# Block products of a SwiGLU layer: two of seven put between ordinary products, side work moved away from the other five

## The chip, the cores and the metric

The kernel runs on one core of one Trainium2 chip. The metric is the device time of one execution in microseconds (us); lower is better.

## The reference

One layer of a decoder, 256 tokens of width 2048, all in 32-bit floats. The change touches only its second half, the feed-forward part:

```python
def swiglu(h, w_ffn_in, w_ffn_out):
    gate, up = jnp.split(h @ w_ffn_in, 2, axis=-1)
    return (jax.nn.silu(gate) * up) @ w_ffn_out
...
    mod = jax.nn.silu(c) @ w_ada[l] + b_ada[l]
    shift1, scale1, gate1, shift2, scale2, gate2 = jnp.split(mod[:, None, :], N_MOD, axis=-1)
...
    h = rms_norm(x, norm2_gain[l]) * (1 + scale2) + shift2
    x = x + gate2 * swiglu(h, w_ffn_in[l], w_ffn_out[l])
```

The inner width D_FF is 5632: w_ffn_in is 2048 by 11264 (5632 gate columns, then 5632 up columns), w_ffn_out is 5632 by 2048. `gate2`, one of six modulation vectors, is a product of one row with a large matrix and is computed beside the feed-forward part.

## The kernel before

**Matrix products.** Every float is split into a high and a low half that TensorE takes (`fp32r`), and a product is made of three matmuls (`mm3`): high weights with high activations (L170), low weights with high activations (L171), high weights with low activations (L172). Weights move in tiles of two chunks of 128 rows by 512 columns, 512 KB. One tile goes through three steps: a load on SyncE's queue (L159, `raw_tile`, into a ring of four `raw` buffers, with two more, tags A4 and A8, in FFN-in, or four, H4 to H7, in FFN-out); a cast on ACT to the high half (L166, `whi`); a subtraction on DVE for the low half (L167, `wlo`). `whi` and `wlo` are rings of four, so that a new half can be made when TensorE has done with the one four tiles earlier. `block` multiplies chunks k0 to k1 into two banks, one for each tile of 128 tokens (`NT` = 2): twelve matmuls for each weight tile.

**FFN-in.** The loop runs over i=0 to 10 (`NFF` = 11). Each step makes 512 gate columns (`pg`, two banks) and 512 up columns (`pu`, two banks) from 16 chunks of 128 (`KC`). In step 0 all of it is ordinary. From i=1 on the first four chunks of gate and up together are done as a 2x2 block product in seven products in place of eight, `right_sums` for the weights' side and `chain` for the rest. With c11, c21 the two token tiles of the gate and c12, c22 those of up, the products stand in this order, each of six matmuls: P1 into c11 (weights b11); P2 into a bank of its own, `side` (t1 = b12-b11); after them ACT copies c11 to c21 (L1268) and `side` to `held` (L1271); P3 into c21 (t2 = b22-t1); DVE sets c12 = c21 + held (L1252); P4 into c11 (b21); P5 into c21 (b22-b12); DVE sets c22 = c21 + held (L1252); P6 into c12 (b22); P7 into c21 (b21-t2). On the activations' side the sums (`h2_sums`, `total`) are ready. Then `block` adds chunks 4 to 15 of the gate to pg, ACT takes Silu (L1307), `block` adds chunks 4 to 15 of up to pu, and DVE multiplies the two (L1315). I call the part from P1 to Silu the gate half, the rest the up half.

**FFN-out.** Four column blocks of 512 (n=0 to 3) over 44 chunks (`KF`), in pairs n=0/1 and n=2/3. The first eight chunks of a pair are two groups of block products (`act_sums`, two entries), so that each of the seven products has twelve matmuls; the rest is ordinary.

**Side work**, in three kinds. Transposes: each step's product of gate and up is turned for FFN-out by `turn` (eight transposes on TensorE, L1071; a cast on ACT, L190; a subtraction on DVE, L191), kept in `later` and issued in the next step between P5 and P6; `block` would issue it as well, when it comes to its chunk `DEFER` = 4 with `later` filled. The second gate's multiply-adds: a tile of 128 by 1024 of `ada_rest` is loaded by SP (L371) into a ring of three buffers (tags AR0, AR1, KC) and added by DVE (L287), 32 of them; then the bias rows (`rows_of`: loads of `b_ada`, L935, into a ring `scr` of three; DVE, L936; high and low halves in T6, L945 and L946; matmuls with a row of ones, L950/L951; a copy, L952). These are steps of a generator, which `tick` advances: `block` calls `tick(state["rate"])` once a weight tile, and the rate is RATE_FFN = 0.4 all through FFN-in. Left sums: at i=8 and 9 (`LATE`) the sums of activations that FFN-out's block products need (`left_sums`, L1207 to L1214, on DVE but for a cast on ACT).

**What sets the order.** The program is written in order and a scheduler orders each engine's queue by priorities. `prio()` moves what stands in it ahead by `AHEAD` = 4000 places, so the weights' loads, casts and low halves go as early as their buffers allow. `tc.issue_after(x)` keeps an instruction behind x. Each engine then works its list strictly in order.

Of the kernel before, what the change touches and what calls it, by code (L numbers as in the profile page):

```python
# [67 lines left out]
def trunk(ctx: ExitStack, tc: tile.TileContext, I, out):  # L68
# [16 lines left out]
    def S(tag, shape, dtype=F32):  # L85
        return slot.tile(shape, dtype, tag=tag, name=nm(tag))
# [1130 lines left out]
    def right_sums(src, b0, b1, places):  # L1217
# [6 lines left out]
        def differ(tag, x, y):  # L1224
            d = S(tag, [P, 2, NB])
            nc.vector.tensor_tensor(d, x, y, op=ALU.subtract)
            return d

        out = []
        with prio():  # L1230
            raws = [(raw_tile(src, 4 * g, b0), raw_tile(src, 4 * g, b1)) for g in range(len(places))]
            raws = [r + (raw_tile(src, 4 * g + 2, b0), raw_tile(src, 4 * g + 2, b1)) for g, r in enumerate(raws)]
            out += [halved(b11) for b11, b12, b21, b22 in raws]
            t1 = [differ(p[0], r[1], r[0]) for p, r in zip(places, raws)]
            out += [halved(t) for t in t1]
            t2 = [differ(p[1], r[3], t) for p, r, t in zip(places, raws, t1)]
            out += [halved(t) for t in t2]
            out += [halved(r[2]) for r in raws]
            out += [halved(differ(p[0], r[3], r[1])) for p, r in zip(places, raws)]
            out += [halved(r[3]) for r in raws]  # L1240
            for t, r in zip(t2, raws):
                nc.vector.tensor_tensor(t, r[2], t, op=ALU.subtract)
            out += [halved(t) for t in t2]
        return out

    def chain(lefts, sums, rights, c11, c21, c12, c22):

        side, held = misc_bank([P, NB]), scr([P, NB])
# [5 lines left out]
        rights = iter(rights)  # L1254

        def product(ps, left, first=False):
            for g in range(len(sums)):
                hi, lo = next(rights)
                for i in range(2):
                    h, l = left(g, i)  # L1260
                    begin, end = first and g == i == 0, g == len(sums) - 1 and i == 1
                    mm3(ps, h, l, hi[:, i, :], lo[:, i, :], begin, end, seeded=True)

        total = lambda q: lambda g, i: (sums[g][0][:, q, i, :], sums[g][1][:, q, i, :])
        part = lambda c, t: lambda g, i: lefts(4 * g + c + i, t)
# [11 lines left out]
        if later:  # L1277
            with tc.issue_after(state["mm"].ins), prio():
                later.pop()()
        product(c12, total(3))  # L1280
        product(c21, part(2, 1))
# [148 lines left out]
```

## Time and profile before

| | |
|---|---|
| median of 3 runs | 1637.32 us (1631.86 to 1638.42) |
| profiled execution | 1637.97 us, span 1636.2 us |
| granted TensorE clock, mean | 0.991 |
| TensorE busy | 1598.8 us, 98% of the span, 7269 instructions |
| DVE busy | 1240.3 us, 76%, 1418 instructions |
| ACT busy | 854.5 us, 52%, 1180 instructions |
| GpSimd busy | 5.3 us |
| read from memory | 393.71 MB, 243 GB/s over the span |

Busy TensorE time is the time in which any matmul was on its way; matmuls overlap, so that a busy engine need not be at its peak, and the distance between starts tells more. A row of the profile's timeline gives start, length, engine, line, operation, output <- inputs, shape, count, and in brackets the idle time ahead with what ended it. Lines are those of this kernel; in the changed kernel those from L1307 on are four higher.

### The profile page before, as it was taken

The numbers are of one execution on the slowest core, as the hardware profiler recorded it, in microseconds if no ns is written. First come the engines' busy times: TensorE is split into PE (matmuls) and PEld (weight loads), VectorE is DVE, ScalarE is ACT, GpSimd is POOL, SyncE is SP. The second block draws the span as 40 slices with busy tenths as digits, with TensorE's granted clock in tenths as the row PEclk, the third lists the DMA queues.
The fourth block names the chain that finished last, engine by engine and source line by source line (L and its number), as shares of the span: only waits on it lengthen the run. The fifth ranks groups of instructions, "written<-read, shape, count | busy, mean of one in ns | idle before, by whom it ended". The sixth has DMA issues, their size and how long they took to land.

```text
span 1636.2 us, 20051 instructions
## 1 busy us (share of the span) xinstructions
PE 1598.8 (98%) x7269; PEld 1313.2 (80%) x7269; DVE 1240.3 (76%) x1418; ACT 854.5 (52%) x1180; POOL 5.3 (0%) x14
## 2 busy tenths in 40 slices
PE   8999999999999999999999999999999998999999
PEld 7878888788777888888887887888787786788787
DVE  6889996878779787878757778888888775755754
ACT  5654458755677444444445555555555553544532
POOL 1000000000000000000000000000000000000000
PEclk9999999999999999999999999999999998999999
DMA  8999996875767889888676577777775566666653
GB/s 332 352 327 319 328 314 210 295 249 151 237 217 242 276 304 312 304 309 305 223 217 220 155 256 239 244 259 239 263 224 184 172 205 223 198 202 181 206 155 114
DMA packets 116179, 399.24 MB, mean 244 GB/s; under 512 B 13090, under 2 KB 13896, under 8 KB 116080
## 3 DMA queue, kind: packets, MB, share of 16 engines
q1 hardware_dynamic: 115856, 397.95, 73.7%
q8 instruction: 57, 0.93, 0.2%
q14 instruction: 42, 0.34, 0.1%
q0 software_dynamic: 224, 0.01, 0.0%
HBM read 393.71 MB, written 4.19 MB: 243 GB/s over the span
## 4 chain that ended last, share of the span: by engine, by line
PE 87%; DVE 6%; DMA 3%; ACT 2%; issue 1%; POOL 0%; DVEq 0%; ACTq 0%; POOLq 0%
PE acc L172 26%; PE acc L171 26%; PE acc L170 26%; DVE wlo L167 3%; DMA AR<-ada_rest 1%; ACT whi L166 1%; PE acc L430 1%; PE misc L786 1%; PE misc L170 1%; PE misc L171 1%; PE misc L1071 1%; PE misc L172 1%; DVE ada L287 1%; DMA raw<-w_in 0%; PE misc L423 0%
## 5 line engine op out<-in xcount | busy, mean ns | idle before, releaser
L166 ACT CAST whi<-raw 128x1024 fp32r<-128x1024 f32 (+1 forms) x449 | 459.9, 1027 | 486.8 <-PE acc L172 376.7
L167 DVE TENSOR_TENSOR wlo<-raw,whi 128x1024 fp32r<-128x1024 f32 (+1 forms) x449 | 531.4, 1191 | 233.0 <-ACT whi L166 231.2
L171 PE MATMUL acc<-wlo,H 128*128 128x512 f32 x1476 | 579.2, 392 | 6.1 <-DVE wlo L167 6.0
L172 PE MATMUL acc<-whi,H 128*128 128x512 f32 x1476 | 578.5, 392 | 0.9 <-DVE H L1157 0.5
L170 PE MATMUL acc<-whi,H 128*128 128x512 f32 x1476 | 577.0, 392 | 0.8 <-ACT H L1156 0.4
L171 PEld LDWEIGHTS acc<-wlo,H 128*128 128x128 f32 x1476 | 278.2, 188 | 66.9 <-DVE wlo L167 10.5
L172 PEld LDWEIGHTS acc<-whi,H 128*128 128x128 f32 x1476 | 278.2, 189 | 59.6 <-DVE H L449 1.8
L170 PEld LDWEIGHTS acc<-whi,H 128*128 128x128 f32 x1476 | 278.3, 189 | 58.3 <-ACT H L442 1.2
L166 ACT CAST whi<-A 128x1024 fp32r<-128x1024 f32 x98 | 103.0, 1054 | 94.8 <-PE acc L172 86.5
L170 PE MATMUL acc<-whi,A 128*128 128x512 f32 x332 | 131.4, 397 | 7.6 <-ACT whi L166 5.6
L167 DVE TENSOR_TENSOR wlo<-A,whi 128x1024 fp32r<-128x1024 f32 x98 | 118.7, 1218 | 24.1 <-ACT whi L166 24.1
L171 PE MATMUL acc<-wlo,A 128*128 128x512 f32 x332 | 129.9, 391 | 0.0
L172 PE MATMUL acc<-whi,A 128*128 128x512 f32 x312 | 122.6, 393 | 0.0
L287 DVE SCALAR_TENSOR_TENSOR ada<-AR,csil,ada 128x1024 f32<-128x1024 f32 x59 | 74.9, 1279 | 8.1 <-DMA AR<-ada_rest 8.1
L170 PEld LDWEIGHTS acc<-whi,A 128*128 128x128 f32 x332 | 62.6, 189 | 22.3 <-ACT whi L166 6.1
L166 ACT CAST whi<-H 128x1024 fp32r<-128x1024 f32 x41 | 43.0, 1053 | 64.0 <-PE acc L172 39.4
L167 DVE TENSOR_TENSOR wlo<-H,whi 128x1024 fp32r<-128x1024 f32 x41 | 49.8, 1221 | 35.0 <-ACT whi L166 34.9
L171 PEld LDWEIGHTS acc<-wlo,A 128*128 128x128 f32 x332 | 62.6, 189 | 12.6 <-DVE wlo L167 0.4
L172 PEld LDWEIGHTS acc<-whi,A 128*128 128x128 f32 x312 | 59.2, 190 | 12.4
L171 PE MATMUL acc<-wlo,T 128*128 128x512 f32 x120 | 46.7, 389 | 0.0
L170 PE MATMUL acc<-whi,T 128*128 128x512 f32 x120 | 46.7, 389 | 0.0
L172 PE MATMUL acc<-whi,T 128*128 128x512 f32 x120 | 46.7, 389 | 0.0
(407 smaller groups left out, 1560.4 us busy)
## 6 DMA issues: line engine op xcount, KB each, us to landing
raw<-w_in SPq DMA_DIRECT2D x203, 512.0 KB, 4.9
raw<-w_ffn_in SPq DMA_DIRECT2D x122, 512.0 KB, 4.4
AR<-ada_rest SPq DMA_DIRECT2D x79, 512.0 KB, 4.8
A<-w_ffn_in SPq DMA_DIRECT2D x54, 512.0 KB, 4.7
raw<-w_ffn_out SPq DMA_DIRECT2D x53, 512.0 KB, 4.2
H<-w_ffn_out SPq DMA_DIRECT2D x35, 512.0 KB, 4.0
raw<-w_out SPq DMA_DIRECT2D x32, 512.0 KB, 4.6
KC<-ada_rest SPq DMA_DIRECT2D x30, 512.0 KB, 5.3
```

Of the source, the lines that this page charges most:

```text
L166: nc.scalar.copy(hi, raw)
L167: state["split"] = nc.vector.tensor_tensor(lo, raw, hi.bitcast(F32), op=ALU.subtract)
L170: nc.tensor.matmul(ps, lh, rh, start=start, stop=False, skip_group_check=seeded)
L171: nc.tensor.matmul(ps, lh, rl, start=False, stop=False, skip_group_check=seeded)
L172: state["mm"] = nc.tensor.matmul(ps, ll, rh, start=False, stop=stop, skip_group_check=seeded)
L287: nc.vector.scalar_tensor_tensor(acc, raw, c, acc, op0=ALU.mult, op1=ALU.add)
L430: state["warm"] = nc.tensor.matmul(ps, ones_r, wide, start=True, stop=True)
L786: nc.tensor.matmul(ps[:n, t * N_GLA + h, :].rearrange("p (s l) -> p s l", l=L), at(f, h, t)[:, :n], odd(at(f, h, t)), start=True, stop=True,)
L1071: nc.tensor.transpose(ps[:, i, :], src[:, i * P : (i + 1) * P], ident)
```

## The change

`paired` takes the place of `right_sums` and `chain`. The first five products stand as before. P6 and P7 each get an ordinary weight tile of the gate ahead of them: chunks 4 and 5, P6, chunks 6 and 7, P7, then chunks 8 to 15. In FFN-out with its two groups each of the four half products gets one: chunks 8 and 9 to 14 and 15. The transposes are no longer issued between P5 and P6; the last `block` of `paired` issues them when it has done four chunks, so behind chunks 8 to 11. The rate of the side work is 0.8 a weight tile within `paired` for i below 7 (six tiles a step), 1.6 from i=7 on, and 0 in the up half; before it was 0.4 for twelve tiles. The left sums come after all of `paired` in the program. As the rate is doubled from i=7, all of the last bias rows' work falls in i=7 to 9. The number of matmuls and of DVE, ACT and SP instructions stays what it was.

```diff
@@ -1214,55 +1214,55 @@
         nc.vector.tensor_tensor(lo, raw, hi.bitcast(F32), op=ALU.subtract)
         return hi, lo
 
-    def right_sums(src, b0, b1, places):
+    def paired(act, sums, places, src, b0, b1, p0, p1, k1):
+
+        (c11, c21), (c12, c22) = p0, p1
+        n = len(sums)
+        side, held = misc_bank([P, NB]), scr([P, NB])
 
         def halved(raw):
             hi, lo = halves_room()
             halve(hi, lo, raw)
             return hi, lo
 
-        def differ(tag, x, y):
-            d = S(tag, [P, 2, NB])
+        def differ(x, y, tag=None, into=None):
+            d = S(tag, [P, 2, NB]) if into is None else into
             nc.vector.tensor_tensor(d, x, y, op=ALU.subtract)
             return d
 
-        out = []
         with prio():
-            raws = [(raw_tile(src, 4 * g, b0), raw_tile(src, 4 * g, b1)) for g in range(len(places))]
+            raws = [(raw_tile(src, 4 * g, b0), raw_tile(src, 4 * g, b1)) for g in range(n)]
             raws = [r + (raw_tile(src, 4 * g + 2, b0), raw_tile(src, 4 * g + 2, b1)) for g, r in enumerate(raws)]
-            out += [halved(b11) for b11, b12, b21, b22 in raws]
-            t1 = [differ(p[0], r[1], r[0]) for p, r in zip(places, raws)]
-            out += [halved(t) for t in t1]
-            t2 = [differ(p[1], r[3], t) for p, r, t in zip(places, raws, t1)]
-            out += [halved(t) for t in t2]
-            out += [halved(r[2]) for r in raws]
-            out += [halved(differ(p[0], r[3], r[1])) for p, r in zip(places, raws)]
-            out += [halved(r[3]) for r in raws]
-            for t, r in zip(t2, raws):
-                nc.vector.tensor_tensor(t, r[2], t, op=ALU.subtract)
-            out += [halved(t) for t in t2]
-        return out
-
-    def chain(lefts, sums, rights, c11, c21, c12, c22):
-
-        side, held = misc_bank([P, NB]), scr([P, NB])
+            first = [halved(r[0]) for r in raws]
+            t1 = [differ(r[1], r[0], p[0]) for p, r in zip(places, raws)]
+            first += [halved(t) for t in t1]
+            t2 = [differ(r[3], t, p[1]) for p, r, t in zip(places, raws, t1)]
+            first += [halved(t) for t in t2]
+            first += [halved(r[2]) for r in raws]
+            first += [halved(differ(r[3], r[1], p[0])) for p, r in zip(places, raws)]
+        rest = []
+        for q in range(2 * n):
+            g, k = q % n, 4 * n + 2 * q
+            w = load_weights(src, k, k + 2, b0)
+            with prio():
+                rest.append((w, halved(raws[g][3] if q < n else differ(raws[g][2], t2[g], into=t2[g]))))
 
         def add(dst):
             with prio(2 * AHEAD):
                 nc.vector.tensor_tensor(dst, c21, held, op=ALU.add)
 
-        rights = iter(rights)
-
-        def product(ps, left, first=False):
-            for g in range(len(sums)):
-                hi, lo = next(rights)
-                for i in range(2):
-                    h, l = left(g, i)
-                    begin, end = first and g == i == 0, g == len(sums) - 1 and i == 1
-                    mm3(ps, h, l, hi[:, i, :], lo[:, i, :], begin, end, seeded=True)
+        def times(ps, left, right, g, start=False):
+            hi, lo = right
+            for i in range(2):
+                h, l = left(g, i)
+                mm3(ps, h, l, hi[:, i, :], lo[:, i, :], start and i == 0, i == 1, seeded=True)
+
+        def product(ps, left, start=False):
+            for g in range(n):
+                times(ps, left, first.pop(0), g, start and g == 0)
 
         total = lambda q: lambda g, i: (sums[g][0][:, q, i, :], sums[g][1][:, q, i, :])
-        part = lambda c, t: lambda g, i: lefts(4 * g + c + i, t)
+        part = lambda c, t: lambda g, i: act(4 * g + c + i, t)
         product(c11, part(0, 0), True)
         with prio(2 * AHEAD):
             nc.scalar.copy(c21, c11)
@@ -1274,11 +1274,14 @@
         product(c11, part(2, 0))
         product(c21, total(2))
         add(c22)
-        if later:
-            with tc.issue_after(state["mm"].ins), prio():
-                later.pop()()
-        product(c12, total(3))
-        product(c21, part(2, 1))
+        for q, (w, right) in enumerate(rest):
+            k = 4 * n + 2 * q
+            block(p0, act, None, k, k + 2, 0, w=w, go_on=True, more=True, seeded=True)
+            if q < n:
+                times(c12, total(3), right, q)
+            else:
+                times(c21, part(2, 1), right, q - n)
+        block(p0, act, src, 8 * n, k1, b0, go_on=True, seeded=True)
 
     for i in range(NFF):
         pg = [acc_bank() for _ in range(NT)]
@@ -1290,12 +1293,13 @@
             pu = [acc_bank() for _ in range(NT)]
         else:
             pu = [acc_bank() for _ in range(NT)]
-            chain(h2_at, h2_sums, right_sums(w_ff, i, NFF + i, [("A13", "A14")]), *pg, *pu)
+            state["rate"] = (2 if i < 7 else 4) * RATE_FFN
+            paired(h2_at, h2_sums, [("A13", "A14")], w_ff, i, NFF + i, pg, pu, KC)
+            state["rate"] = 0.0
             if i in LATE:
                 assert not macs
                 with prio():
                     act_sums.append(left_sums(LATE[i], ("A13", "A14"), *act[i - min(LATE)]))
-            block(pg, h2_at, w_ff, 4, KC, i, go_on=True, seeded=True)
         sgs = []
         with prio():
             for t in range(NT):
```

In FFN-out `chain(act_at, act_sums, rights, *both[0], *both[1])` becomes `paired(act_at, act_sums, [("A13", "A14"), ("H2", "H3")], w_fo, n, n + 1, *both, KF)`, and the `block` for the rest of n=0 and n=2 that stood there is now the last line of `paired`.

Three places show the order. First DVE where the up half of i=4 ends and the products of i=5 come near. `wlo` are low halves, L1226 (L1230 in the changed kernel) the differences of weights, L1315 (L1319) the two multiplies that end step 4. Before:

```order
L1226 TENSOR_TENSOR A_2024_9489<-A_2018_9477,A_2021_9483 128x1024
L167 TENSOR_TENSOR wlo_9382<-raw_9379,whi_9381 128x1024
L287 SCALAR_TENSOR_TENSOR ada_7984<-AR_1984_9265,csil,ada_7984 128x1024
L167 TENSOR_TENSOR wlo_9480<-raw_9471,whi_9479 128x1024
L287 SCALAR_TENSOR_TENSOR ada_7984<-AR_1985_9304,csil,ada_7984 128x1024
L167 TENSOR_TENSOR wlo_9486<-A_2021_9483,whi_9485 128x1024
L1226 TENSOR_TENSOR A_2029_9499<-A_2018_9477,raw_9473 128x1024
L167 TENSOR_TENSOR wlo_9492<-A_2024_9489,whi_9491 128x1024
L1315 TENSOR_TENSOR scr_9345<-scr_9345,acc_9121 128x512
L1315 TENSOR_TENSOR scr_9347<-scr_9347,acc_9122 128x512
```

After:

```order
L167 TENSOR_TENSOR wlo_9388<-raw_9385,whi_9387 128x1024
L1230 TENSOR_TENSOR A_2026_9491<-A_2020_9479,A_2023_9485 128x1024
L167 TENSOR_TENSOR wlo_9482<-raw_9473,whi_9481 128x1024
L167 TENSOR_TENSOR wlo_9488<-A_2023_9485,whi_9487 128x1024
L1230 TENSOR_TENSOR A_2031_9501<-A_2020_9479,raw_9475 128x1024
L167 TENSOR_TENSOR wlo_9494<-A_2026_9491,whi_9493 128x1024
L1319 TENSOR_TENSOR scr_9351<-scr_9351,acc_9121 128x512
L1319 TENSOR_TENSOR scr_9353<-scr_9353,acc_9122 128x512
```

The two multiply-adds (L287) are gone from here, and t2's difference (into A_2024, now A_2026) stands one place later; the rest stands in the same order.

Then DVE among the products of i=5, from the low half of b21 on; acc_9469 is c12, acc_9470 c22, acc_9468 c21. Before:

```order
L167 TENSOR_TENSOR wlo_9496<-raw_9475,whi_9495 128x1024
L167 TENSOR_TENSOR wlo_9502<-A_2029_9499,whi_9501 128x1024
L1252 TENSOR_TENSOR acc_9469<-acc_9468,scr_9515 128x512
L167 TENSOR_TENSOR wlo_9506<-A_2018_9477,whi_9505 128x1024
L167 TENSOR_TENSOR wlo_9511<-A_2024_9489,whi_9510 128x1024
L1252 TENSOR_TENSOR acc_9470<-acc_9468,scr_9515 128x512
L167 TENSOR_TENSOR wlo_9579<-A_2040_9576,whi_9578 128x1024
L191 TENSOR_TENSOR T_2010_9464<-misc_9550,A_2009_9463 128x4x128
L191 TENSOR_TENSOR T_2010_9464<-misc_9557,A_2009_9463 128x4x128
L167 TENSOR_TENSOR wlo_9585<-raw_9582,whi_9584 128x1024
```

After:

```order
L167 TENSOR_TENSOR wlo_9498<-raw_9477,whi_9497 128x1024
L167 TENSOR_TENSOR wlo_9504<-A_2031_9501,whi_9503 128x1024
L1252 TENSOR_TENSOR acc_9469<-acc_9468,scr_9472 128x512
L167 TENSOR_TENSOR wlo_9510<-A_2034_9507,whi_9509 128x1024
L167 TENSOR_TENSOR wlo_9514<-A_2020_9479,whi_9513 128x1024
L1252 TENSOR_TENSOR acc_9470<-acc_9468,scr_9472 128x512
L167 TENSOR_TENSOR wlo_9520<-raw_9517,whi_9519 128x1024
L167 TENSOR_TENSOR wlo_9525<-A_2026_9491,whi_9524 128x1024
L287 SCALAR_TENSOR_TENSOR ada_7984<-KC_9281,csil,ada_7984 128x1024
L167 TENSOR_TENSOR wlo_9607<-raw_9604,whi_9606 128x1024
L167 TENSOR_TENSOR wlo_9613<-raw_9610,whi_9612 128x1024
L287 SCALAR_TENSOR_TENSOR ada_7984<-AR_1985_9308,csil,ada_7984 128x1024
```

Up to c22's sum the order is the same but for which weights the last two low halves are of: A_2034 is chunks 4 and 5, A_2020 b22 (before: b22, then b21-t2). Behind it stand chunks 6 and 7 (raw_9517), b21-t2, and the multiply-adds; the transposed block's subtractions (L191) have left.

Last TensorE at the end of P5 in i=5; acc_9467 is c11. Before:

```order
L170 MATMUL acc_9468<-whi_9501,A_1710_8063 128x512
L171 MATMUL acc_9468<-wlo_9502,A_1710_8063 128x512
L172 MATMUL acc_9468<-whi_9501,A_1711_8064 128x512
L1071 MATMUL misc_9550<-ident,scr_9345 128x128 x4
L1071 MATMUL misc_9557<-ident,scr_9347 128x128 x4
L170 MATMUL acc_9469<-whi_9505,A_1710_8063 128x512
L171 MATMUL acc_9469<-wlo_9506,A_1710_8063 128x512
L172 MATMUL acc_9469<-whi_9505,A_1711_8064 128x512
```

After:

```order
L170 MATMUL acc_9468<-whi_9503,A_1710_8063 128x512
L171 MATMUL acc_9468<-wlo_9504,A_1710_8063 128x512
L172 MATMUL acc_9468<-whi_9503,A_1711_8064 128x512
L170 MATMUL acc_9467<-whi_9509,H_1607_7511 128x512
L171 MATMUL acc_9467<-wlo_9510,H_1607_7511 128x512
L172 MATMUL acc_9467<-whi_9509,H_1611_7515 128x512
L170 MATMUL acc_9467<-whi_9509,H_1607_7511 128x512
L171 MATMUL acc_9467<-wlo_9510,H_1607_7511 128x512
L172 MATMUL acc_9467<-whi_9509,H_1611_7515 128x512
L170 MATMUL acc_9468<-whi_9509,H_1607_7511 128x512
L171 MATMUL acc_9468<-wlo_9510,H_1607_7511 128x512
```

Behind P5's last matmuls come no transposes and no P6 into acc_9469, but the ordinary tile of chunks 4 and 5, six matmuls into c11 and six into c21.

More of the change, by code (lines that the diff above doesn't have):

```diff
@@ L1352, in trunk @@
             both = [[acc_bank() for _ in range(NT)] for _ in range(2)]
-            rights = right_sums(w_fo, n, n + 1, [("A13", "A14"), ("H2", "H3")])
-            chain(act_at, act_sums, rights, *both[0], *both[1])
+            paired(act_at, act_sums, [("A13", "A14"), ("H2", "H3")], w_fo, n, n + 1, *both, KF)
         pss = both[n % 2]
@@ L1375, in trunk @@
         else:
-            block(pss, act_at, w_fo, K0, KF, n, go_on=True, seeded=True)
+            if n == 1:
+                block(pss, act_at, w_fo, K0, KF, n, go_on=True, seeded=True)
             if n == 0:
```

## The prediction

> **What bounds the kernel now.** I read the chain of waits first, then a table of stretches: one for each of the ten steps of the FFN-in loop that hold block products (i=1 to 10), two for FFN-out (n=0/1 and n=2/3). Its columns: stretch, length, busy us and instructions of PE, PEld, DVE, ACT, POOL, granted clock, DMA share, GB/s. Last come TensorE's waits in FFN-in (total us, times, longest) and one of them.
>
> ```profile
> PE 87%; DVE 6%; DMA 3%; ACT 2%; issue 1%; POOL 0%; DVEq 0%; ACTq 0%; POOLq 0%
> ```
> ```profile
> 936.48:979.54 43.06, 43.06 (x195) 35.75 (x194) 34.26 (x34) 22.85 (x25) 0.00 (x0) 1.00 0.73 237
> 979.54:1023.96 44.42, 43.68 (x195) 35.59 (x194) 36.41 (x35) 22.53 (x25) 0.00 (x0) 1.00 0.74 249
> 1023.96:1067.01 43.05, 43.05 (x195) 35.75 (x194) 34.92 (x33) 22.85 (x25) 0.00 (x0) 1.00 0.76 246
> 1067.01:1111.27 44.26, 43.67 (x195) 35.59 (x194) 36.78 (x36) 22.84 (x25) 0.00 (x0) 1.00 0.77 250
> 1111.27:1155.01 43.74, 43.44 (x195) 35.59 (x194) 35.55 (x34) 22.84 (x25) 0.00 (x0) 1.00 0.75 249
> 1155.01:1199.98 44.97, 43.99 (x195) 35.51 (x194) 36.55 (x35) 22.52 (x25) 0.00 (x0) 1.00 0.74 244
> 1199.98:1244.41 44.43, 43.40 (x195) 35.67 (x194) 35.93 (x37) 23.24 (x26) 0.00 (x0) 1.00 0.67 209
> 1244.41:1290.20 45.79, 43.87 (x195) 35.51 (x194) 36.35 (x39) 23.88 (x26) 0.00 (x0) 1.00 0.60 186
> 1290.20:1335.21 45.01, 43.62 (x197) 35.90 (x196) 34.55 (x37) 24.18 (x27) 0.00 (x0) 1.00 0.59 187
> 1335.21:1378.59 43.38, 43.38 (x198) 36.03 (x197) 25.40 (x27) 21.81 (x26) 0.00 (x0) 1.00 0.73 241
> 1378.59:1512.60 134.01, 126.60 (x549) 103.21 (x548) 85.21 (x82) 60.87 (x65) 0.00 (x0) 0.96 0.62 188
> 1512.60:1636.20 123.60, 117.50 (x517) 95.83 (x515) 68.69 (x66) 48.00 (x47) 0.00 (x0) 0.98 0.51 158
> ```
> ```profile
> PE acc L171 <- DVE wlo L167: 5.0, 7, 1.6
> PE acc L170 <- DVE acc L1252: 2.0, 4, 1.0
> ```
> ```profile
> 1193.05 1.28 DVE L287 SCALAR_TENSOR_TENSOR ada<-AR,csil,ada 128x1024 f32<-128x1024 f32 x1
> 1194.24 1.22 DVE L167 TENSOR_TENSOR wlo<-raw,whi 128x1024 fp32r<-128x1024 f32 x1
> ...
> 1206.65 0.50 PE L170 MATMUL acc<-whi,A 128*128 128x512 f32 x1 [1.03 <-DVE acc L1252]
> ```
> ```profile
> 1302.66 0.50 PE L171 MATMUL acc<-wlo,H 128*128 128x512 f32 x1 [1.39 <-DVE wlo L167]
> ```
>
> TensorE is the bound: in i=1, 3 and 10 it is busy for the whole step. Steps of 195 matmuls without a gap take 43.05 us, others up to 2.74 more. DVE, at 25 to 37 us of 43, is not short of time but late in places. At i=7 a multiply-add (1.19 us of DVE, 1193.05 to 1194.24), two more like it and the up half's low halves have put it behind, and P5 waits for c12's sum. At i=9 the first ordinary block waits for a low half, since the left sums stand between. The waits that are named add to 7.0 us.
>
> What can go is read from lengths, since a wait also delays matmuls that the list doesn't name. i=1 to 9 sum to 398.73 us; nine steps of 43.05 are 387.45; the 11.28 over, less some 0.25 for i=9's two extra matmuls, leave **11.0 us**.
>
> **The change part by part.** The pattern to copy is the step that was clean with no multiply-add before it, i=10. P1 starts at 1335.24.
>
> ```profile
> 1334.99 1.28 DVE L1315 TENSOR_TENSOR scr<-scr,acc 128x512 f32<-128x512 f32 x2
> 1335.24 0.39 PE L170 MATMUL acc<-whi,H 128*128 128x512 f32 x1
> 1336.19 1.22 DVE L1242 TENSOR_TENSOR A<-A,A 128x1024 f32<-128x1024 f32 x1
> 1337.32 2.35 DVE L167 TENSOR_TENSOR wlo<-A,whi 128x1024 fp32r<-128x1024 f32 x2
> 1339.60 0.69 DVE L1252 TENSOR_TENSOR acc<-acc,scr 128x512 f32<-128x512 f32 x1
> 1340.20 1.21 DVE L167 TENSOR_TENSOR wlo<-raw,whi 128x1024 fp32r<-128x1024 f32 x1
> 1341.33 1.22 DVE L167 TENSOR_TENSOR wlo<-A,whi 128x1024 fp32r<-128x1024 f32 x1
> 1341.81 0.40 PE L172 MATMUL acc<-whi,A 128*128 128x512 f32 x1
> 1342.05 1.04 PE L1071 MATMUL misc<-ident,scr 128*128 128x128 f32 x8
> 1342.46 0.69 DVE L1252 TENSOR_TENSOR acc<-acc,scr 128x512 f32<-128x512 f32 x1
> 1342.84 0.48 PE L170 MATMUL acc<-whi,A 128*128 128x512 f32 x1
> ```
>
> The 30th matmul, P5's last, stands at 1341.81: 6.57 us for 29 steps, 0.2266 each, 1.36 a product of six, 2.72 an ordinary block of twelve. DVE takes 1.13 for a low half or difference (1340.20 to 1341.33), 0.60 for a sum (1339.60 to 1340.20), 1.20 for the two multiplies, 0.79 of PE for eight transposes (1342.05 to 1342.84). No matmul is added or removed, and PE's work stays the same.
>
> *Multiply-adds out of the up half.* With none there, DVE enters every block-product region as at i=10. That removes the lateness of P4 and P5 in i=4 to 8.
>
> *Interleaving, and the transposes moved.* Up to c22's sum DVE's order is the one above, with k=4's low half in b22's place and b22's in the last one's. So c22's sum ends at 1342.46+0.69, that is 7.91 us after P1 starts. Now a new wait: before, c21 was next written by P7; now the block k=4,5 writes it, behind six matmuls into c11, at 36×0.2266=8.16. It would overwrite c21 while the sum reads it, so it waits for the sum: 0.25 to spare. Behind that I walked DVE on: k=6's low half ends at about 9.1 (PE wants it at 10.9), P7's at 10.2 (13.6), a multiply-add, k=8 at 12.5 (15.0), k=10 at 13.7 (17.7). Before, PE ran P6 and P7 straight behind the transposes and came to k=4 after 3.5 us, while DVE still had splits or left sums in hand; now each product has a block of 2.72 ahead of it. Cost 0; this removes the block waits of i=2, 6, 8 and 9. The left sums of i=8 and 9 now stand behind P7's low half: L1207's 1.13 makes k=8 at 12.5 there as well. The splits of the transposed block (two instructions, about 1.2) go from the tight place to one with leads above 2 us.
>
> *Multiply-adds into the gate half.* Its DVE work: multiplies 1.2, one difference and ten low halves 11×1.13=12.4, sums 1.2, splits 1.2, 4.8 multiply-adds 5.7: 21.7 us, against PE's 7×1.36+6×2.72+0.79=26.6. The 4.9 us left are the lead with which the up half begins. Cost 0, covered by that lead. Their loads:
>
> ```profile
> AR<-ada_rest SPq DMA_DIRECT2D x79, 512.0 KB, 4.8
> ```
>
> The ring has three buffers. The first is free after the first multiply-add (11.4 on my clock) and wanted again at 18.3 by the fourth: 6.9 us for a load of 4.8. Cost 0, though the load is put in behind SP's weight loads.
>
> *Twice the rate from i=7.* There the four small b_ada loads (second gate's bias rows) come up together, three of them behind a wait for a scratch buffer, among weight loads on SP; DVE's L936 then stands ahead of the up half's low halves. Before, one went out 0.4 us behind a weight load:
>
> ```profile
> 1227.94 0.33 SPq L159 DMA_DIRECT2D raw<-w_ffn_in  x1
> 1228.32 0.28 SPq L935 DMA_DIRECT2D scr<-b_ada  x1
> 1232.57 0.67 DVE L936 TENSOR_TENSOR ada<-ada,scr 1x512 f32<-1x512 f32 x1
> ```
>
> It was used 4.25 us after its issue. If each goes like that, DVE's lead of 4.9 covers it, and it costs 0. If one lands only after four weight loads (4×0.524 MB at 249 GB/s, the rate of i=2, 8.4 us), it comes 4.2 later; two of them one after the other 8.4, which is 3.5 past the lead. I take 0.5, near the lower end, since the only row of such a load is there.
> The Trainium skill, "DMA: Bandwidth & Descriptors", section "Two DMAs through the same engine are not ordered", states that descriptors of one queue on one engine start in order; by that the small load stands behind every weight load put in before it, and the term would be the 3.5 rather than the 0.5. The row of 4.25 us does not contradict it, as only one weight load stood close ahead.
>
> *Bias rows' matmuls* (L950/L951) move from i=10 and FFN-out into i=8 and 9, where their low halves (L946) come just in time: 0 to 2 us, and I take 0.2, as the same chain in i=10 ended no wait.
>
> *FFN-out.* The order of n=0/1 and n=2/3 changes likewise. What is lost there:
>
> ```profile
> PE acc L170 <- ACT whi L166: 7.7, 5, 5.6
> PE acc L171 <- DVE wlo L167: 1.6, 2, 0.8
> ```
> ```profile
> 1386.01 0.79 PE L170 MATMUL acc<-whi,A 128*128 128x512 f32 x1 [5.64 <-ACT whi L166]
> ...
> 1388.40 0.63 PE L170 MATMUL acc<-whi,A 128*128 128x512 f32 x1
> 1388.83 0.63 PE L171 MATMUL acc<-wlo,A 128*128 128x512 f32 x1
> ```
>
> The 5.64 us is a wait for a weight buffer that FFN-in's last block still held, and the clock is low behind it (0.43 a matmul against 0.2266). Same buffers and same order now: it stays. So do the gaps ahead of P5, as DVE has three differences and their low halves in a row there, before and now. Gain 0 to 4; I take 0.
>
> Sum: −11.0+0.5+0.2 = **−10.3 us** on the profiled execution, 1637.97 us (span 1636.2). Its median of runs is 0.65 lower, so 1627.7 there is 1627.0 as a median.
>
> **Rivals.**
>
> A. *The new wait on c22's sum is not met.* If DVE enters one instruction late (1.13 to 1.20), c21's block starts 0.9 late, in ten steps 9 us: 1636. For it: only 0.25 us to spare, and P5 was late by this cause at i=4 to 8. Against: at i=1, 3 and 10 no gap, two of them with multiply-adds in the step. It decides from 0.25 us of lateness on.
>
> B. *The bias loads cost in full.* 3.5 us instead of 0.5, and the matmuls' 2 instead of 0.2: 1627.0+4.8=1631.8, inside 0.5%. For it: four such loads and one chain of bias rows fall in a step and a half. Against: the row of 4.25 us.
>
> C. *Slower: the bunched multiply-adds starve.* A load of ada_rest that takes more than 6.9 us stops DVE, and TensorE once 4.9 more are used up. To end 0.5% slower the seven steps i=1 to 7 must give back 10.3 and 8.2 more, 2.6 each: loads of 14.4 us, against a median of 4.8. At 15 us each: 1627.0+7×3.2=1649. Little speaks for it; DMA's share is 0.75 in these steps, which makes a tail likely, though not threefold.
>
> D. *The change does not reach the waits.* P4's and P5's lateness may come from the differences and low halves around the step's start, which keep their order, with the multiply-adds only a part of it. i=4, 5 and 7 (1.21, 0.69 and 1.38 over 43.05) wait at these products alone; with a part of i=6 and 8 that is about 4 of the 11, which would stay: 1631. For it: i=3 has multiply-adds and no gap. Against: i=10, with the same order and none.
>
> **How the numbers follow.** What a measurement of this kernel can tell from no change is about 0.5%, 8.2 us: faster is below 1629.1, slower above 1645.5. The forecast has 0.53 (1623 to 1629.5: the FFN-out gaps' 4 below, some of the small terms above), A 0.14, B 0.14, D 0.13, C 0.06. Faster: nearly all of the forecast and a part of B and D, 0.57; slower: C, 0.06; same 0.37. The low end is 1627.0 less 4, with 1 for the spread of runs: 1622; the high end takes in A: 1636.
>
> **What would show it.** In the changed profile each of i=1 to 7 takes 43.1 us, i=8 and 9 some 43.9 with their extra matmuls; TensorE's waits for L167 and L1252 in FFN-in are gone; c22's sum ends 7.9 us after P1 starts, and no matmul into c21 names it. A gap of about 1 us 8.2 us after each P1 shows A; DVE idle on b_ada at i=7 shows B, DVE idle on ada_rest C, gaps at P4 and P5 that stay D. I am wrong most easily in the 0.25 us of c21, and in FFN-out, which I leave as it is.

## The result, and the profile after

| | before | changed |
|---|---|---|
| median | 1635.85 us (1631.86 to 1638.42, 6 runs) | 1624.74 us (1621.32 to 1629.16, 6 runs) |
| profiled execution | 1637.97 us, span 1636.2 | 1626.09 us, span 1624.3 |

The ratio is 0.9937, with a 95% interval from 0.9914 to 0.9959: 0.6% faster, 11.1 us between the medians and 11.9 between the profiled executions.

The stretches of the changed kernel, cut at the same places (P1 of i=1 to i=10, then n=0/1 and n=2/3):

```profile
935.76:978.85 43.09, 43.09 (x196) 35.74 (x194) 35.60 (x35) 22.86 (x25) 0.00 (x0) 1.00 0.74 256
978.85:1021.96 43.11, 43.11 (x196) 35.75 (x195) 35.03 (x33) 22.85 (x25) 0.00 (x0) 1.00 0.74 244
1021.96:1065.23 43.27, 43.27 (x196) 35.59 (x194) 36.85 (x36) 22.85 (x25) 0.00 (x0) 1.00 0.78 255
1065.23:1108.32 43.09, 43.09 (x196) 35.74 (x195) 36.71 (x35) 22.85 (x25) 0.00 (x0) 1.00 0.78 257
1108.32:1151.42 43.10, 43.10 (x195) 35.74 (x194) 36.58 (x35) 22.85 (x25) 0.00 (x0) 1.00 0.77 256
1151.42:1194.49 43.07, 43.07 (x196) 35.74 (x194) 36.50 (x35) 22.84 (x25) 0.00 (x0) 1.00 0.79 256
1194.49:1237.57 43.08, 43.08 (x196) 35.74 (x194) 36.83 (x38) 23.25 (x26) 0.00 (x0) 1.00 0.63 196
1237.57:1281.60 44.03, 44.03 (x201) 36.38 (x200) 35.49 (x39) 25.29 (x30) 0.00 (x0) 1.00 0.63 191
1281.60:1325.87 44.27, 44.27 (x203) 36.61 (x202) 35.83 (x40) 26.06 (x32) 0.00 (x0) 1.00 0.63 191
1325.87:1369.00 43.13, 43.13 (x196) 35.80 (x195) 24.91 (x25) 21.21 (x24) 0.00 (x0) 1.00 0.73 242
1369.00:1501.00 132.00, 124.69 (x539) 101.54 (x538) 82.76 (x76) 58.12 (x58) 0.00 (x0) 0.97 0.61 188
1501.00:1624.30 123.30, 116.35 (x517) 94.79 (x515) 69.81 (x68) 47.89 (x47) 0.00 (x0) 1.00 0.52 162
```

In all nine steps i=1 to 9 TensorE is now busy from end to end, and the list of its waits there is empty. Their sum is 390.11 us where it was 398.73: 8.6 of the 11.9. i=8 and 9 are about 1 us longer than the others, by six and eight more matmuls, the bias rows'. i=10 gives 0.25 and n=0/1 2.0, with ten matmuls fewer; n=2/3 gives 0.3, and 0.7 lies ahead of i=1, where nothing is changed. Two of the bias rows' sixteen matmuls still stand in i=10, so their work does not all fall in i=7 to 9, as the section on the change has it.

The new wait, at i=5 (P1 at 1108.32), on DVE and on TensorE:

```profile
1115.54 0.69 DVE L1252 TENSOR_TENSOR acc<-acc,scr 128x512 f32<-128x512 f32 x1
...
1116.48 0.39 PE L170 MATMUL acc<-whi,H 128*128 128x512 f32 x1
```

c22's sum ends at 1116.23, 7.91 after P1, and the first matmul into c21 starts at 8.16, as foreseen. At i=3 (P1 at 1021.96) DVE is 0.28 behind, and that shows how little room there is: c22's sum starts at 1029.46 and ends at 1030.15, 8.19 after P1; the matmul starts at 1030.20, which is 8.24 and not 8.16 after P1, and the step takes 43.27.

The small bias loads at i=7, on SP and DVE:

```profile
1212.97 0.33 SPq L159 DMA_DIRECT2D raw<-w_ffn_in  x1
1213.56 0.24 SPq L935 DMA_DIRECT2D scr<-b_ada  x1
...
1215.53 0.24 SPq L935 DMA_DIRECT2D scr<-b_ada  x1
...
1217.48 0.33 SPq L159 DMA_DIRECT2D raw<-w_ffn_in  x1
1217.90 0.25 SPq L935 DMA_DIRECT2D scr<-b_ada  x1
1218.57 1.27 DVE L936 TENSOR_TENSOR ada<-ada,scr 1x512 f32<-1x512 f32 x2
...
1223.34 0.67 DVE L936 TENSOR_TENSOR ada<-ada,scr 1x512 f32<-1x512 f32 x1
```

The two additions of 1218.57 use the loads of 1213.56 and 1215.53, that of 1223.34 the load of 1217.90. The load of 1213.56, 0.6 behind a weight load, is used 5.0 us after its issue; that of 1215.53 is used 3.6 later (the second addition starts at 1219.2); that of 1217.90, 0.4 behind a weight load, 5.4 later. Neither row of additions has idle time ahead, so the loads had landed by then at the latest. The step takes 43.08.

FFN-out keeps its waits:

```profile
PE acc L170 <- ACT whi L166: 8.9, 7, 5.8
```

With two smaller rows TensorE waits 10.3 us there, where it was 9.5.

### The profile page after: what moved, and what is told of

It reads as the page before. It is cut to its first block, busy times and chain, and to the rows that moved or that the text cites. A ratio compares the mean times of both kernels' runs of the same rounds, so it can differ in the third digit from the quotient of the medians.

```text
span 1624.3 us, 20044 instructions
## 1 busy us (share of the span) xinstructions
PE 1592.4 (98%) x7269; PEld 1311.2 (81%) x7269; DVE 1242.4 (76%) x1418; ACT 855.2 (53%) x1180; POOL 5.4 (0%) x14
## 4 chain that ended last, share of the span: by engine, by line
PE 89%; DVE 4%; DMA 3%; ACT 2%; issue 1%; POOL 0%; DVEq 0%; ACTq 0%; POOLq 0%
PE acc L172 27%; PE acc L171 27%; PE acc L170 27%; DVE wlo L167 2%; ACT whi L166 1%; PE misc L1071 1%; DMA H<-w_ffn_out 1%; PE acc L430 1%; DMA AR<-ada_rest 1%; PE misc L786 1%; DMA raw<-w_ffn_out 1%; PE misc L170 1%; PE misc L171 1%; PE misc L172 1%; DMA raw<-w_in 0%
## 5 line engine op out<-in xcount | busy, mean ns | idle before, releaser
L287 DVE SCALAR_TENSOR_TENSOR ada<-AR,csil,ada 128x1024 f32<-128x1024 f32 x59 | 75.1, 1279 | 6.8 <-DMA AR<-ada_rest 6.8
L167 DVE TENSOR_TENSOR wlo<-H,whi 128x1024 fp32r<-128x1024 f32 x41 | 49.9, 1223 | 34.2 <-ACT whi L166 29.2
```

The lines of the kernel that those rows point to most:

```text
L167: state["split"] = nc.vector.tensor_tensor(lo, raw, hi.bitcast(F32), op=ALU.subtract)
L287: nc.vector.scalar_tensor_tensor(acc, raw, c, acc, op0=ALU.mult, op1=ALU.add)
```

## The experiments

The steps are compared by the length of i=1 to 9 in one row, with columns as above. P1 to P7 are the products; "lateness" is a wait of TensorE. The edits are against the kernel before or the changed one.

**New rates alone.** Against the kernel before:

```diff
+            state["rate"] = (2 if i < 7 else 4) * RATE_FFN
             chain(h2_at, h2_sums, right_sums(...), *pg, *pu)
...
             block(pg, h2_at, w_ff, 4, KC, i, go_on=True, seeded=True)
+            state["rate"] = 0.0
```

> The kernel before, with only the rate of the side work changed (0.8 or 1.6 in the gate half, 0 in the up half); products, transposes and left sums stand where they stood. The measure is the sum of the steps i=1 to 9 in the profile: 398.7 us before, 390.1 after. Theory 1 (three separate causes, each a place in DVE's list: multiply-adds ahead of the products at i=4, 5, 7 and a part of 8, 3.7 us; the difference b21-t2 behind c12's sum at i=2 and 6, 3.2 us; left sums ahead of k=4's low half at i=8 and 9, 3.4 us): DVE's list without multiply-adds in the up half has the difference ahead in every step, so the first two causes go and the third stays: i=1 to 7 at 43.1 us each, i=8 and 9 with gaps of 1.5 to 1.8 at the first ordinary block; sum about 393.5, whole time about 0.45% below before. Rival (the interleaving is what counts: P6, P7 and k=4 straight behind P5 outrun DVE with the transposed block's subtractions among them): P7 and k=4 still wait 0.5 to 1.2 in several of i=1 to 7; sum 396 to 398, within 0.2% of before.

Measured: 1637.66 us, ratio 0.9998 (0.9985 to 1.0012). No gain at all.

```profile
935.68:1334.69 399.01, 392.44 (x1761) 322.61 (x1760) 323.99 (x318) 211.83 (x238) 0.00 (x0) 1.00 0.71 228
```

Theory 1 missed; the rival has the time about right, but not the place: P7 and k=4 don't wait in i=1 to 7. i=2 and 3 are clean, as theory 1 has it, but at i=4 to 7 P4 and P5 together wait 0.6 to 1.2 us a step, with no multiply-add ahead of them. The cause of the wait at i=5 stands 10 to 30 us earlier, in i=4 (P1 at 1064.88), on SP and DVE:

```profile
1086.20 1.52 SPq L371 DMA_DIRECT2D AR<-ada_rest  x2
1089.72 0.33 SPq L371 DMA_DIRECT2D KC<-ada_rest  x1
1090.15 0.38 SPq L159 DMA_DIRECT2D raw<-w_ffn_in  x1
1092.71 2.66 SPq L371 DMA_DIRECT2D AR<-ada_rest  x2
1095.47 0.86 SPq L159 DMA_DIRECT2D raw<-w_ffn_in  x2
1096.38 2.51 SPq L159 DMA_DIRECT2D A<-w_ffn_in  x2
```
```profile
1102.98 1.23 DVE L1226 TENSOR_TENSOR A<-raw,raw 128x1024 f32<-128x1024 f32 x1 [4.45 <-DMA raw<-w_ffn_in]
```
```profile
1114.90 0.50 PE L171 MATMUL acc<-wlo,H 128*128 128x512 f32 x1 [0.81 <-DVE wlo L167]
```

DVE stands 4.45 us for the next products' weights: L1226 is t1's difference, b12-b11. SP issued b11 at 1090.15, but b12 only at 1095.47, 30.6 us after P1, behind five loads of ada_rest; P4 pays for it at 1114.90. The multiply-adds are late by a line that the change does not touch: `mac` issues each behind the low half made last in the program (`tc.issue_after(state["split"].ins)`, L356). In an uncut `block` of six tiles that is the low half of chunk 14. In `paired` the part is cut in three calls, so that the first multiply-adds stand behind P7's low half.

**The changed kernel with the old rates** (its two `state["rate"]` lines out).

> The changed kernel with the rate of the side work set back to 0.4 in both halves; the interleaved products, late transposes and late left sums stay. Theory 1: the multiply-adds at the end of the up half make DVE late again at P4 and P5 in i=3 to 8, about 4 us in all, and c22's sum with it; TensorE has then already waited at P5, so c21's block adds at most 0.1 to 0.3 a step. Sum of i=1 to 9 about 394 to 395 (390.1 after), whole time 0.25% to 0.3% above the changed kernel. The difference b21-t2 is needed 5 us later than before, so no wait at P7. Rival A of the prediction (c21's new wait costs one DVE instruction a step once DVE is late): another 0.9 in each late step, sum 398 or more, as slow as before. Rival (interleaving alone is the gain): sum 391.

Measured: 1631.16 us, ratio 0.9964 (0.9952 to 0.9976).

```profile
934.80:1329.50 394.70, 391.14 (x1750) 320.99 (x1748) 322.71 (x312) 208.09 (x229) 0.00 (x0) 1.00 0.71 231
```
```profile
PE acc L170 <- DVE acc L1252: 3.1, 6, 0.9
```

Theory 1 holds: the sum is 4.6 us above the changed kernel's, with eleven of the bias rows' matmuls fewer in it (about 0.16 us each, by i=8 and 9 above), so that some 6 us of waits are back. The six waits for a sum are at P5 in i=2 to 7, and none is at c21's block: where DVE is late, P5 has waited for it already, and c21's block comes later by as much. Rival A of the prediction priced this wait wrongly.

**Transposes back between P5 and the next block.**

```diff
         add(c22)
+        if later:
+            with tc.issue_after(state["mm"].ins), prio():
+                later.pop()()
```

> The changed kernel with the transposes issued between P5 and the block of k=4 and 5 again. Theory 1: the transposed block's subtractions then stand behind P7's low half on DVE (end at 11.4 us after P1's start, k=8's low half at 12.5 to 13.7 against a need at 15.0), and c21's block comes 0.8 later, so no wait: i=1 to 7 at 43.1 us, sum of i=1 to 9 within 0.5 of 390.1, no difference in time. Rival (moving the transposes is needed, since 1.2 us of DVE and 2 us of ACT fall among the products): waits at P7 or k=8 of 0.5 to 1 us in most steps, sum 394 to 398.

Measured: 1627.17 us, ratio 0.994 (0.9922 to 0.9959).

i=1 to 9 take 390.17 us. The late place of the transposes is worth nothing here.

**P6 and P7 straight behind P5.**

```diff
-        for q, (w, right) in enumerate(rest):
...
+        product(c12, total(3))
+        product(c21, part(2, 1))
+        block(p0, act, src, 4 * n, 8 * n, b0, go_on=True, more=True, seeded=True)
         block(p0, act, src, 8 * n, k1, b0, go_on=True, seeded=True)
```

> The changed kernel with P6 and P7 straight behind P5 as before; rates, late transposes and late left sums stay. Theory 1 (the interleaving itself buys nothing, the three causes were the other work on DVE): k=4's low half ends 9.1 us after P1's start against a need at 9.5 to 10.0, no wait; sum of i=1 to 9 within 0.7 of 390.1, no difference in time to the changed kernel. Rival (interleaving is what gives DVE its lead): k=4's block waits 0.5 to 1 us in each step, sum 395 to 399.

Measured: 1626.67 us, ratio 0.994 (0.9919 to 0.996).

i=1 to 9 take 389.82 us, with TensorE busy throughout. Nor is the interleaving, the edit that gives the change its name, worth anything as long as the rest stays: the rates, the late left sums, and a `block` that is still cut in two.

**New rates and a cut call**, products, transposes and left sums as before:

```diff
-            block(pg, h2_at, w_ff, 4, KC, i, go_on=True, seeded=True)
+            block(pg, h2_at, w_ff, 4, 8, i, go_on=True, more=True, seeded=True)
+            block(pg, h2_at, w_ff, 8, KC, i, go_on=True, seeded=True)
```

> The kernel before with the new rates, as in the first experiment, and the ordinary part of the gate half cut into two calls (chunks 4 to 7, 8 to 15); P6 and P7 behind P5, transposes between P5 and P6, left sums early. In the first experiment DVE waited 4.4 us in the up half of i=4 for a weight load, and SP had put the loads of ada_rest at 1086 to 1095 us, ahead of it; in the changed kernel they are out by 1088 on the same clock. Theory 2 (what counts is how early in the gate half the multiply-adds stand, since their loads hold up the next products' weights on SP; cutting the call moves them two weight tiles ahead): i=1 to 7 at 43.1 to 43.3 us, i=8 and 9 still with a wait of 1.3 to 1.6 for the left sums; sum of i=1 to 9 about 393 (399.0 uncut, 390.1 changed kernel), time 0.3% to 0.45% below before. Rival (the transposes among the products make DVE late): P4 and P5 of i=4 to 7 still wait 0.5 to 1.5, sum 397 to 399.

Measured: 1629.68 us, ratio 0.9944 (0.9926 to 0.9963).

```profile
935.14:1327.74 392.60, 390.08 (x1762) 323.17 (x1760) 324.79 (x318) 211.80 (x238) 0.00 (x0) 1.00 0.71 232
```

One cut takes 6.4 us from the first experiment: i=1 to 7 take 43.05 to 43.08 each, with the transposes among the products. The next products' weights now go out earlier (the P1 of i=4 is within 0.6 us of the first experiment's):

```profile
1086.16 2.66 SPq L371 DMA_DIRECT2D AR<-ada_rest  x2
1088.92 2.36 SPq L159 DMA_DIRECT2D raw<-w_ffn_in  x4
1094.10 2.57 SPq L159 DMA_DIRECT2D A<-w_ffn_in  x2
```

All four raw tiles are issued by 1091.3, where the first experiment began its last two at 1095.47. b12 goes out 25.5 us after P1 in place of 30.6, and t1's difference starts 33.4 after it in place of 38.1. The raw tiles do not land sooner: their median is 7.8 us in this step, 7.4 in the first experiment. So it is the time of their issue that counts here, and that follows the multiply-adds: the first of i=4 starts 13.6 us after P1 in place of 20.0. TensorE has two waits left, 2.5 us together, the left sums'.

**Loads of ada_rest by GpSimd**, with the new rates and the uncut call:

```diff
-                    nc.sync.dma_start(raw, w_ada[...])
+                    nc.gpsimd.dma_start(raw, w_ada[...])
```

(in FFN-in only).

> The kernel of the first experiment (new rates alone, uncut call) with the second gate's loads of ada_rest issued by GpSimd in place of SP; DVE's list is the same as there. Theory 2 (SP's queue): the weight loads no longer stand behind them, DVE's wait of 4.4 us for a weight load in the up half shrinks below 2, P4 and P5 of i=4 to 7 wait 0 to 0.3; sum of i=1 to 9 about 393 to 394 (the left sums' waits stay). Rival 1 (DVE is late by the bunched multiply-adds themselves): the waits stay at 0.5 to 1.5, sum 399. Rival 2 (the transfers' rate, not the order of issue, is short): DVE still waits for weights, now beside more transfers at once, sum 397 or more.

Measured: 1642.1 us, ratio 1.0031 (1.0021 to 1.0042), 0.3% slower.

```profile
934.11:1339.23 405.12, 394.87 (x1761) 321.99 (x1760) 322.79 (x318) 211.59 (x238) 15.34 (x29) 1.00 0.69 225
```

The time is as rival 2 has it, but that does not clear SP's queue, because DVE's order did not stay as expected. In i=4 (P1 at 1068.33), on DVE and SP:

```profile
1102.54 1.23 DVE L1227 TENSOR_TENSOR A<-raw,raw 128x1024 f32<-128x1024 f32 x1 [2.27 <-DMA raw<-w_ffn_in]
1103.68 2.35 DVE L167 TENSOR_TENSOR wlo<-A,whi 128x1024 fp32r<-128x1024 f32 x2
1104.93 1.46 SPq L159 DMA_DIRECT2D A<-w_ffn_in  x2
1108.67 1.23 DVE L1227 TENSOR_TENSOR A<-A,A 128x1024 f32<-128x1024 f32 x1 [2.63 <-DMA A<-w_ffn_in]
```

In the first experiment the same two low halves stand ahead of t1's difference (L1226 there, at 1102.98):

```profile
1095.07 1.23 DVE L167 TENSOR_TENSOR wlo<-A,whi 128x1024 fp32r<-128x1024 f32 x1
1097.31 1.23 DVE L167 TENSOR_TENSOR wlo<-A,whi 128x1024 fp32r<-128x1024 f32 x1 [1.01 <-ACT whi L166]
```

Off SP's queue, b12 goes out 26.3 us after P1 in place of 30.6, and t1's difference starts 34.2 after it in place of 38.1: the queue did hold the weights back. But the two low halves free A4 and A8, and now they stand behind that difference. So b22's load goes out 36.6 us after P1 in place of 31.5, and t2's difference (1108.67) starts 40.3 us after P1, about as late as before (40.6). How much of the slowdown comes from this order, and how much from transfers side by side, is not shown.

**Short multiply-adds** (128 of 1024 columns), rates and call as in the first experiment.

> The kernel of the first experiment (new rates alone, uncut call), with each of the second gate's multiply-adds, but the first of each half, done on 128 of its 1024 columns; the loads stay whole. It leaves 7/8 of the second gate's sums out. DVE saves about 1.0 us on each of 4 to 5 of them a step. Theory 3 (in the uncut call the multiply-adds stand behind the low halves of all six tiles; DVE's time there makes the up half's low halves late, so the raw buffers come free late, and so the next products' weights): the waits at P4 and P5 of i=4 to 7 go, DVE's wait for a weight load in the up half falls from 4.4 below 1.5, sum of i=1 to 9 about 392 to 393 (399.0 with whole multiply-adds). Rival (the transfers: SP issues the loads of ada_rest late, and they take the rate from the weights): the waits stay at 0.5 to 1.5, sum 397 or more.

Measured: 1630.2 us, one run; the second gate lacks 7/8 of its sums.

```profile
931.58:1328.83 397.25, 392.03 (x1762) 322.60 (x1760) 297.30 (x318) 211.78 (x238) 0.00 (x0) 1.00 0.71 229
```

DVE's busy time falls by 26.7 us, the sum by only 1.8, as the rival has it. The order changed with it (the scheduler put three multiply-adds in a row, and so three loads), and the waits moved to other steps. That speaks against DVE's time alone as the cause.

**Half of each load**, DVE's time kept:

```diff
-                raw = araw([P, 2 * NB])
+                wide = NB if ring["tags"] == ("AR0", "AR1", "KC") else 2 * NB
+                raw = araw([P, wide])
```

> The kernel of the first experiment, with half of each load of ada_rest in FFN-in (512 of 1024 columns), and each multiply-add done in two of 512 columns on the same half, so that DVE's time stays (two of about 0.6 us for one of 1.19). It puts wrong weights into half of the second gate. Theory 3 (DVE's time is what is late): P4 and P5 of i=4 to 7 still wait 0.5 to 1.5 each, sum of i=1 to 9 397 to 399. Rival (transfers): 1.3 MB less in each step, the waits go, sum 392 to 394.

Measured: 1630.52 us, one run; half of the second gate has wrong weights.

```profile
937.93:1330.98 393.05, 390.35 (x1762) 323.05 (x1760) 327.20 (x350) 211.81 (x238) 0.00 (x0) 1.00 0.68 212
```

With DVE 3 us busier than in the first experiment, the waits of i=4 to 7 are gone, and the left sums' two remain, 2.7 us together, again as the rival has it. That points to the loads of ada_rest, and not to DVE's time. By which of their effects is not told apart: with half the bytes the raw tiles of i=4 land in a median of 4.5 us in place of 7.4, but the order moved as well. SP puts the weight loads between those of ada_rest (b12 24.2 us after P1 in place of 30.6), the pairs of half multiply-adds stand a little differently on DVE from the whole ones, and t1's difference stands ahead of the up half's last low halves, as in the sixth experiment. In the fifth the raw tiles take 7.8 us and TensorE does not wait in i=1 to 7, so that slow landing alone does not make the wait.

**Rates, cut call, and left sums behind the last tile**: the fifth experiment with `left_sums` moved below `block`, as in the change.

> As the kernel with new rates and the cut call, and the left sums moved behind the gate half's last tile as in the changed kernel; products and transposes stand as before. If the three causes are multiply-adds and their loads, the difference b21-t2, and left sums, this small edit does all that the change does: sum of i=1 to 9 390 to 390.5, time 0.6% to 0.7% below before, no difference to the changed kernel. If interleaving or the transposes' place has a part of its own, it stays 1 to 4 us above.

Measured: 1627.7 us, ratio 0.9938 (0.9917 to 0.996).

i=1 to 9 take 390.14 us. These three small edits do in FFN-in what the whole change does.

**A later sum.** Two needless instructions ahead of c22's sum in the changed kernel, reading k=4's low half.

> The changed kernel with two needless DVE instructions of 512 columns (0.3 to 0.6 us each) between b22's low half and c22's sum, in i=1 to 8. c22's sum ended 7.91 us after P1's start and c21's block wanted to start at 8.16. If the block waits for the sum, as the prediction has it, its first matmul into c21 comes 0.35 to 0.95 late in each of the eight steps, with c22's sum (L1252) named as what ended the wait; sum of i=1 to 9 393 to 398. Rival (the 0.25 us is no bound, because a first write of c21 does not wait for the sum's end): no wait, sum 390 to 390.5.

Measured: 1626.66 us, one run, i=1 to 9 at 390.13. Inconclusive: the scheduler knew of the later sum and put three of P6's matmuls ahead of those into c21, so that nothing waited. The price of that wait is known only from i=3 above.

**FFN-out's first tiles in other buffers** (a version to beat the change):

```diff
             rooms["extra"] = ("H4", "H5", "H6", "H7")
+            rooms["n"] = 0
...
+            low = [2, 3] if n == 1 else [3, 2]
+            got = [{j: raw_tile(src, 4 * g + 2, (b0, b1)[j - 2]) for j in low} for g in range(n)]
+            raws = [r + (d[2], d[3]) for r, d in zip(raws, got)]
```

> The changed kernel, with FFN-out's first weight tiles given other buffers: n=0's and n=2's b11 and b12 take the raw ring, the other four H4 to H7, b22 ahead of b21, so that no tile of P1 or P2 waits for the buffer that FFN-in's last matmul holds. The wait of 5.9 us ahead of P1 at n=0 should fall below 1, the stretch at half clock behind it (about 2.5 us lost) go, and P3 may wait up to 1 us for t2: 7 to 8.5 us less than the changed kernel, ratio to before 0.988 to 0.990. Rival: the wait only moves to P2 to P4, as H2, H3 and H7 are freed by the same matmul: 2 to 4 us less, 0.991 to 0.993.

Measured: 1620.51 us, ratio 0.9889 (0.9874 to 0.9904).

```profile
PE acc L170 <- ACT whi L166: 3.4, 6, 0.9
PE misc L171 <- DVE wlo L167: 2.2, 2, 1.6
PE acc L171 <- DVE wlo L167: 0.5, 2, 0.4
```

The 5.8 us ahead of P1 is gone, and P2 waits 1.6 for t1's low half. From P1 of i=10 to P1 of n=2 it takes 168.29 us in place of 173.74.

**P5's differences ahead of c12's sum in FFN-out**, on top of that:

```diff
-            with prio(2 * AHEAD):
+            with tc.issue_after(last.ins) if n == 2 and dst is c12 else nullcontext(), prio(2 * AHEAD):
                 nc.vector.tensor_tensor(dst, c21, held, op=ALU.add)
```

where `last` is the second of P5's differences.

> The kernel with FFN-out's first tiles in other buffers, and there P5's two differences of weights put ahead of c12's sum on DVE, where they stood behind it with two low halves to make before P5. P5's waits of 2.4 us (n=0) and 2.5 (n=2) should fall below 0.5 each: 3.5 to 4.5 us less than that kernel, ratio to before 0.986 to 0.9875. Rival: the low halves of b21 for P4, now behind the differences, come late by one or two instructions (1.1 to 2.3 us) and the wait only moves to P4: no gain or up to 1 us.

Measured: 1614.97 us (1614.73 to 1616.5), ratio 0.986 (0.983 to 0.9891): the fastest of all, some 10 us below the changed kernel by the medians.

```profile
PE acc L171 <- DVE wlo L167: 1.5, 3, 0.6
PE misc L171 <- DVE wlo L167: 1.5, 1, 1.5
PE acc L170 <- DVE acc L1258: 0.4, 1, 0.4
```

The 3.4 us of waits for casts, at P5 and right behind it, are gone; besides P2's 1.5 some 1.9 us remain, 0.35 at P3 and the rest at P5: 0.56 at n=0 and 0.96 at n=2, where below 0.5 each was expected.

## Why the prediction was right, and where it was not

The time came out: 1627.0 foreseen, 1624.74 measured, inside the range and faster. The forecast started from 1637.32 for the kernel before, whose median over six runs is 1635.85; as a difference, 10.3 us were foreseen and 11.1 measured. That it came out is in part luck: of the two steps that were to gain the time, one gains nothing, and the other gains only together with the cut calls, which the forecast did not count.

*What can go (11.0).* Right. The nine steps lost 8.62, and took in twelve of the bias rows' matmuls, (44.03−43.08)+(44.27−43.08)−0.25=1.9 us; so 10.5 of waits went, and 0.2 stays at i=3.

*Bias rows (0.2).* In i=8 and 9 they cost 1.9, since the matmuls stand on TensorE's path, but i=10 and n=0/1 got 0.25 and 2.0 shorter. The net is near zero, as taken. Of the 2.0, ten matmuls at 1.9/12=0.16 make 1.6.

*Bias loads (0.5).* They cost 0. The rule of the Trainium skill that would have made it 3.5 ("DMA: Bandwidth & Descriptors", section "Two DMAs through the same engine are not ordered") is not contradicted: the load 0.4 behind a weight load was in use after 5.4 us, the one 0.8 behind another after 3.6. The 8.4 us were not put to the test, since four weight loads never stood close ahead of one: at most three did, ahead of the first small load (1203.93), and DVE came to it only 8.9 us later, without idle time ahead.

*FFN-out (0).* Right in the main: the wait ahead of P1 and those at P5 stayed, 10.3 us of waits where there were 9.5. The 2.0 us that n=0/1 got shorter are the bias rows' for the most part, as above.

*Interleaving, and the transposes moved: "this removes the block waits of i=2, 6, 8 and 9".* Wrong. Undone one by one (third and fourth experiments), and together in the kernel of rates, cut call and late left sums, they changed nothing. The waits of i=2 and 6 came from b21-t2's difference behind c12's sum on DVE:

```profile
983.91 0.70 DVE L1252 TENSOR_TENSOR acc<-acc,scr 128x512 f32<-128x512 f32 x1
...
985.65 1.22 DVE L1242 TENSOR_TENSOR A<-raw,A 128x1024 f32<-128x1024 f32 x1
986.78 0.69 DVE L1252 TENSOR_TENSOR acc<-acc,scr 128x512 f32<-128x512 f32 x1
988.06 1.23 DVE L167 TENSOR_TENSOR wlo<-A,whi 128x1024 fp32r<-128x1024 f32 x1 [0.58 <-ACT whi L166]
```

That is i=2 before (P1 at 979.57): the difference stands behind c12's sum of 983.91, and its low half starts at 8.49 after P1, against 6.09 at i=10. Where the scheduler has no multiply-adds in the up half, it puts the difference first in each step, and in the first experiment i=2 is clean with the transposes in their old place. At i=6 it is the same: the difference starts at 1161.67, behind c12's sum, and its low half 9.07 after P1. The waits of i=8 and 9 came from the left sums: with them moved, 392.60 fell to 390.14.

*Multiply-adds out of the up half, "that removes the lateness of P4 and P5 in i=4 to 8".* Right for the whole change, wrong as a step by itself: the first experiment has it and gains nothing. (i=6 had no such lateness; its two waits stood behind P5.) I priced the bunched loads at 0 by the ring's 6.9 us. That was the multiply-adds' own wait; I left out which weight loads stand behind them on SP. Rival C named this starvation, but looked for it at DVE's multiply-adds with loads of 14 us; it comes at the next products' weights, of which b12 goes out 5 us later than in the fifth experiment and then lands about as slowly as there. The change escapes the wait because its calls are cut, which I had read as a mere consequence of the interleaving.

*Rival A* was not met; its price was wrong where DVE is late before P5 (second experiment). *Rival D* did not come in the changed kernel; the gaps at P4 and P5 in the first experiment look like it, but come from the late weight loads.

## What to carry to other kernels

When background work hangs on "behind the last thing emitted", the grain of the calls sets where it runs: at the new rates, cutting one call in two was worth 6.4 us here, and the edit that looked like the idea was worth none. Price background loads by which loads stand behind them on the same queue and who waits for those, not by their own ring. When an experiment moves one thing, read the other engines' order again before the time is put down to it. Before crediting a restructuring, try its parts alone: rates without the cut gained nothing, rates with it gained all but the left sums' share.

## What was not expected of the hardware

The raw tiles of i=4 landed in a median of 4.9 us in the kernel before, 7.4 in the first experiment, 7.8 in the fifth and 6.9 in the changed kernel, though each has five loads of ada_rest in that step; with these loads halved it was 4.5. What makes the difference was not looked into. The 6.1 us by which the nine steps grew when GpSimd issued the loads of ada_rest (405.12 against 399.01) are no figure of its queue, since DVE's order changed with it.
